# A gated feed-forward layer: block products of seven in place of eight for part of the K tiles, with their weight sums on GpSimd

## The chip, the cores and the metric

The kernel runs on one core of one Trainium2 chip. The metric is the device time of one execution in microseconds; of several runs the median is given. The engines are named as in the profile: PE is TensorE's matmul, PEld its weight load, DVE is VectorE, ACT is ScalarE, POOL is GpSimd, and SP is the queue that issues most DMAs. A q behind a name (SPq) is the engine's sequencer.

## The reference

One decoder layer over 256 tokens of width 2048, in float32. Two groups of token mixers share one projection; then come a gated feed-forward part, which the change touches, and a gated per-layer embedding:

```python
D_FF = 5632
h = rms_norm(x, mix_norm_g[i]); z = h @ w_in[i]
...
x = x + jnp.concatenate([ha, hb], axis=-1) @ w_out[i]
h = rms_norm(x, ffn_norm_g[i])
u = h @ w_up[i]                      # 2048 x 11264
a, g = jnp.split(u, 2, axis=-1)
a = causal_dwconv(a, conv_w[i], conv_b[i])
x = x + (jax.nn.gelu(a, approximate=False) * g) @ w_down[i]   # 5632 x 2048
gate = jax.nn.sigmoid(rms_norm(x, ple_norm_g[i]) @ w_ple_gate[i])
x = x + gate * (p[i].astype(x.dtype) @ w_ple_proj[i])
```

## The kernel before

Every projection streams its weights once from memory, in blocks of 128 partitions by 1024 columns of float32 (512 KB), which hold two K tiles of 128 rows by 512 columns. A product in float32 is made of three fast products: each operand is split into a rounded part hi and a rest lo, and hi x hi, hi x lo and lo x hi are summed in PSUM. For a weight block, ACT casts hi out of the raw block (line 226), DVE subtracts it to get lo (line 228), and PE multiplies (lines 256 to 258; a weight load and a matmul of 512 columns each). For the activations the split is stored once, hi and lo side by side (`split_T`, lines 141 and 142; with a scale lines 144 and 145).

`run_stream` (line 196) is the loop over the list of blocks. It issues the load of a block on SP, eight blocks ahead in this stage (four raw buffers from the pool `w`, four from `ffn`), makes hi and lo three blocks ahead of PE into four buffers of each, and then calls the block's function. After each block `pull(2)` lets waiting side jobs do two steps. Each engine works through its own queue in order; the framework's scheduler may change the order of independent instructions when the program is built.

`token_group` (line 237) makes the blocks of one group of 512 output columns: eight blocks of two K tiles for the up projection, with two PSUM banks, one for each half of the 256 tokens. A block has 2 halves x 2 K tiles x 3 = 12 matmuls. PSUM's eight banks have two tags, `mm` and `aux`, of four each.

In the feed-forward stage, `up(q)` makes for each of eleven q two groups: 512 columns of a, then the same 512 columns of g. `up_evac` (line 689) takes each bank out on ACT with the norm's scale (line 694) and transposes blocks of 32 on DVE (line 695). After the second group `ffn_job(q)` is queued as a side job. It moves the pieces with 16 DMAs on SP (line 707) so that the columns lie on the partitions, does the convolution on ACT (line 728) and DVE (line 731) with its edges on POOL (lines 719 to 725), the GELU on ACT (line 739), the product with g on DVE (line 743), and splits the result into uT (lines 141 and 142). uT holds 24 of the 44 K tiles. The order is up for q = 0 to 5, down over K tiles 0 to 19, up for q = 6 to 10, down over K tiles 20 to 43, so that the first down part doesn't need the last q made before it. In `down`, before the second last block of the first column group all side jobs are run to their end. The last part's evacuation (`resid`, line 653) adds into the residual xs (line 656), transposes the sum on PE (line 153) and squares it on ACT; the gate's projection follows.

POOL runs the convolution's edges, the root of the norms, and at the start of the kernel memsets and the masks' selects (lines 281 and 290). p is loaded by ACT's queue in the mixers' stage (`load_conv`), and its transpose pT is kept until the end.

## Time and profile before

| what | value |
| --- | --- |
| median of 3 runs | 1273.33 us (1273.25 to 1275.93) |
| the profiled execution's own time | 1273.86 us |
| its span, first to last instruction | 1272.0 us |
| granted TensorE clock | 1.000 |
| matmuls of the feed-forward stage begin | 445.8 us (up), 707.9 us (down) |
| their last one begins | 1167.3 us |
| read from memory | 235.40 MB, 187 GB/s over the span |

The span is divided by busy time of each engine. A row of the groups by line and shape reads: line, engine, operation, what is written from what, shapes, count, then total busy us and mean ns of one, then the engine's idle time before it and what ended it. In the timeline a row begins with its start and its length in us, and neighbouring rows of one kind are merged with their count. A window's row has for each engine the busy us and the number of instructions.

### The profile page before, as it was taken

The page shows a single profiled execution, that of the slowest core. Times are in us where ns is not written, and L with a number is a line of the kernel's source. Part 1 is how long each engine was busy: PE and PEld are TensorE (multiplying, and loading weights), DVE is VectorE, ACT ScalarE, POOL GpSimd, SP SyncE. Part 2 cuts the span into 40 slices and gives each one's busy share as a digit, 9 for nine tenths or more (in the row PEclk, how much of TensorE's full clock was granted, in tenths as well). Part 3 has the DMA queues.
Part 4 walks back from the last instruction along what each step waited for, and adds up shares of the span by engine and source line. Part 5 has one row for each costly group of instructions (what it writes and reads, how often), then busy time and mean ns, then how long its engine had stood idle before and what let it go on. Part 6 is the DMA issues. An engine that isn't in the chain of part 4 may idle for free.

```text
span 1272.0 us, 16250 instructions
## 1 busy us (share of the span) xinstructions
PE 1265.6 (99%) x5964; PEld 1068.6 (84%) x5964; DVE 732.6 (58%) x922; ACT 646.6 (51%) x906; POOL 32.2 (3%) x90
## 2 busy tenths in 40 slices
PE   9999999999999999999999999999999999999998
PEld 7899988888888888888888888888888888888888
DVE  6455555646555555667476655447566656555554
ACT  8655455444655444555455533345455545444443
POOL 2000000000000000000000000000000000000000
PEclk9999999999999999999999999999999999999999
DMA  8566756656555576676576666666667667566661
GB/s 285 159 189 188 227 134 205 198 154 183 149 183 182 191 255 189 219 237 217 173 259 227 207 210 197 193 191 227 190 223 235 215 181 247 185 185 196 206 193 49
DMA packets 163520, 252.21 MB, mean 198 GB/s; under 512 B 28169, under 2 KB 59505, under 8 KB 163441
## 3 DMA queue, kind: packets, MB, share of 16 engines
q1 hardware_dynamic: 162560, 250.72, 62.9%
q8 instruction: 47, 0.77, 0.2%
q10 hardware_dynamic: 657, 0.43, 0.1%
q0 software_dynamic: 224, 0.03, 0.1%
q14 instruction: 32, 0.26, 0.1%
HBM read 235.40 MB, written 2.10 MB: 187 GB/s over the span
## 4 chain that ended last, share of the span: by engine, by line
PE 99%; DMA 0%; SPq 0%; DVE 0%; ACT 0%; issue 0%; DVEq 0%
PE tg L257 32%; PE tg L256 32%; PE tg L258 32%; PE xT L153 1%; PE mob L570 0%; DMA xs<-in_x_dram 0%; PE msc L544 0%; PE ob L489 0%; PE qkp L448 0%; PE sc L464 0%; PE rowb L435 0%; PE pt L483 0%; PE msc L548 0%; PE ob L490 0%; PE sc L463 0%; PE hap L604 0%
## 5 line engine op out<-in xcount | busy, mean ns | idle before, releaser
L228 DVE TENSOR_TENSOR lo<-raw,hi 128x1024 fp32r<-128x1024 f32 (+2 forms) x462 | 545.7, 1183 | 471.6 <-ACT hi L226 467.5
L226 ACT CAST hi<-raw 128x1024 fp32r<-128x1024 f32 (+2 forms) x462 | 469.2, 1017 | 514.0 <-PE tg L258 461.0
L258 PE MATMUL tg<-hi,x2T 128*128 128x512 f32 x704 | 274.1, 389 | 0.0
L257 PE MATMUL tg<-lo,x2T 128*128 128x512 f32 x704 | 274.1, 389 | 0.0
L256 PE MATMUL tg<-hi,x2T 128*128 128x512 f32 x704 | 271.2, 389 | 0.0
L256 PE MATMUL tg<-hi,hT 128*128 128x512 f32 (+1 forms) x512 | 186.7, 368 | 0.0
L257 PE MATMUL tg<-lo,hT 128*128 128x512 f32 (+1 forms) x512 | 186.4, 366 | 0.0
L258 PE MATMUL tg<-hi,hT 128*128 128x512 f32 (+1 forms) x512 | 185.9, 366 | 0.0
L256 PEld LDWEIGHTS tg<-hi,x2T 128*128 128x128 f32 x704 | 132.2, 188 | 27.4
L258 PEld LDWEIGHTS tg<-hi,x2T 128*128 128x128 f32 x704 | 132.2, 188 | 27.3
L257 PEld LDWEIGHTS tg<-lo,x2T 128*128 128x128 f32 x704 | 132.2, 188 | 27.3
L257 PE MATMUL tg<-lo,uT 128*128 128x512 f32 x352 | 137.1, 389 | 0.0
L256 PE MATMUL tg<-hi,uT 128*128 128x512 f32 x352 | 137.0, 390 | 0.0
L258 PE MATMUL tg<-hi,uT 128*128 128x512 f32 x352 | 136.9, 389 | 0.0
L257 PEld LDWEIGHTS tg<-lo,hT 128*128 128x128 f32 x512 | 96.3, 188 | 12.6
L256 PEld LDWEIGHTS tg<-hi,hT 128*128 128x128 f32 x512 | 95.9, 188 | 12.3
L258 PEld LDWEIGHTS tg<-hi,hT 128*128 128x128 f32 x512 | 95.9, 188 | 12.1
L258 PEld LDWEIGHTS tg<-hi,uT 128*128 128x128 f32 x352 | 66.1, 188 | 13.7
L257 PEld LDWEIGHTS tg<-lo,uT 128*128 128x128 f32 x352 | 66.1, 188 | 13.6
L256 PEld LDWEIGHTS tg<-hi,uT 128*128 128x128 f32 x352 | 66.1, 188 | 13.5
L257 PE MATMUL tg<-lo,x3T 128*128 128x512 f32 (+1 forms) x160 | 55.5, 347 | 0.0
L258 PE MATMUL tg<-hi,x3T 128*128 128x512 f32 (+1 forms) x160 | 55.5, 347 | 0.0
(207 smaller groups left out, 963.7 us busy)
## 6 DMA issues: line engine op xcount, KB each, us to landing
raw<-in_w_up_dram SPq DMA_DIRECT2D x176, 512.0 KB, 4.3
raw<-in_w_down_dram SPq DMA_DIRECT2D x88, 512.0 KB, 4.7
raw<-in_w_in_dram SPq DMA_DIRECT2D x79, 512.0 KB, 4.2
raw<-in_w_in_dram SPq DMA_DIRECT2D x48, 344.0 KB, 3.5
raw<-in_w_out_dram SPq DMA_DIRECT2D x32, 512.0 KB, 4.3
raw<-in_w_ple_gate_dram SPq DMA_DIRECT2D x32, 512.0 KB, 4.4
Y<-sq SPq DMA_DIRECT2D x176, 64.0 KB, 2.0
xs<-in_x_dram SPq DMA_DIRECT2D x8, 256.0 KB, 7.5
```

The source lines that it names most:

```text
L153: pe.transpose(bk[:, t * P : (t + 1) * P], xs[:, t, k * P : (k + 1) * P], ident)
L226: act.copy(hi[:, :w], raw[:, :w])
L228: dve.tensor_sub(lo[:, :w], raw[:, :w], f32(hi[:, :w]))
L256: pe.matmul(o, ah, hi[:, i, :], start=first, stop=False)
L257: pe.matmul(o, ah, lo[:, i, :], start=False, stop=False)
L258: pe.matmul(o, al, hi[:, i, :], start=False, stop=last)
```

## The change

The up projection is now made in groups of 1024 columns, 512 of a and 512 of g, and the down projection in two groups of 1024. Of such a group, the two token halves, the two column halves and two neighbouring K tiles make a product of 2 x 2 blocks by 2 x 2 blocks. For some pairs of K tiles it is made of seven block products instead of eight (Strassen's scheme in Winograd's form): for the pairs 1, 3 and 5 of 8 in up, and for the second of the two pairs of every q in down. A step called R is one K tile done in the old way, with four outputs (12 matmuls). A pair done in the new way has four steps: o1 (two block products, from the second raw tile as it came), o2 (one, 512 columns), c1 (two) and c2 (two), 21 matmuls in all. Between o2 and c1, POOL makes lo of the 512 columns of o2 and then four sums of 512 columns in place in the pair's two raw tiles, each sum building on earlier ones; c1 takes hi and lo of the first raw tile, c2 of the second.

The four outputs of a group use four banks (D11 to D22), and the products that go into several outputs four more (Q1, Q5, Q6, Q7). After the last c2, `combine` forms the sums of the Q banks on ACT and DVE into four tiles; in up these are scaled on ACT, and at the end DVE adds each D bank with its scale and transposes. The activations need differences of blocks as well: x2E for up (made at the start by POOL, ACT and DVE), and for down four more units per q, which POOL computes. The product with g moves from DVE to POOL.

hi and lo have five buffers of each, four steps ahead of PE, and raw has seven. uT holds four q of eleven units each. The order is now up for q = 0 to 3, down over them, up and down for 4 to 7, up and down for 8 to 10. A down part needs its last q's new units at the step o1 of the last pair; all side jobs are run to their end before that step of the first column group. p is loaded and transposed at the last down group, into the place of x2E.

```diff
-RAW_FFN = 4
-QF = 24
+RAW_FFN = 3
+PARTS_FFN = 1
+S_UP = (1, 3, 5)
+QW = 4
...
+    def halves(raw, w, eng=None):
...
+        act.copy(hi[:, :w], raw[:, :w])
+        last["hi"] = traced()
+        (eng or dve).tensor_tensor(out=lo[:, :w], in0=raw[:, :w], in1=f32(hi[:, :w]), op=ALU.subtract)
+        return hi, lo
...
+    def quad_group(src, seq, unit, tags, mid, end):
...
+                    pe.matmul(st[bk], ah, hi[:, cols], start=first, stop=False)
+                    pe.matmul(st[bk], ah, lo[:, cols], start=False, stop=False)
+                    pe.matmul(st[bk], al, hi[:, cols], start=False, stop=final)
+                    if final and bk[0] == "D":
+                        end(int(bk[1]) - 1, int(bk[2]) - 1, st[bk])
...
+            if kind == "R":
+                p, i = divmod(p, 2)
+                ops = [(f"D{t + 1}{n + 1}", (p, f"{t + 1}{i + 1}"), n) for t in range(NT) for n in range(2)]
+                step = add(ops, [src(2 * p + i)], lambda raws: halves(raws[0], BLK))
+                step.frees = [(step, 0)]
+            elif kind == "o1":
+                opened[p] = step = add([("D12", (p, "E3"), 1), ("D11", (p, "12"), 0)], [src(2 * p), src(2 * p + 1)],
+                                       lambda raws: halves(raws[1], BLK))
+            elif kind == "o2":
+                def split(_, step=opened[p]):
+                    r0, r1 = step.raws
+                    hl = halves(r0, 512, pool)
+                    for dst, oth in ((r0[:, 0:512], r0[:, 512:1024]), (r0[:, 512:1024], r1[:, 512:1024]),
+                                     (r1[:, 512:1024], r0[:, 0:512]), (r1[:, 0:512], r1[:, 512:1024])):
+                        pool.tensor_tensor(out=dst, in0=dst, in1=oth, op=ALU.add)
+                    return hl
+                add([("Q1", (p, "11"), 0)], split=split)
+            elif kind == "c1":
+                add([("Q5", (p, "E5"), 0), ("Q7", (p, "E7"), 1)],
+                    split=lambda _, step=opened[p]: halves(step.raws[0], BLK), frees=[(opened[p], 0)])
+            else:
+                add([("Q6", (p, "E6"), 1), ("D21", (p, "22"), 0)],
+                    split=lambda _, step=opened[p]: halves(step.raws[1], BLK), frees=[(opened[p], 1)], after=closed)
...
+        def combine(st, tiles):
+            t12, t21, t22 = (tiles(c) for c in ("12", "21", "22"))
+            act.copy(t22, st["Q1"])
+            dve.tensor_sub(t21, st["Q6"], t22)
+            dve.tensor_add(t12, st["Q5"], t21)
+            dve.tensor_add(t21, st["Q7"], t21)
+            dve.tensor_add(t22, st["Q7"], t12)
+            return t12, t21, t22
...
             for f in range(4):
-                dve.tensor_mul(u[:, f], c[:, :, :, f].rearrange("p i t r -> p t i r"),
-                               g[:, :, :, f].rearrange("p i t r -> p t i r"))
+                pool.tensor_tensor(out=u[:, f].rearrange("p t (i r) -> p t i r", i=4),
+                                   in0=c[:, :, :, f].rearrange("p i t r -> p t i r"),
+                                   in1=g[:, :, :, f].rearrange("p i t r -> p t i r"), op=ALU.mult)
...
+            differences(e, u[:, 2, 0], u[:, 3, 0], u[:, 2, 1], u[:, 3, 1])
...
-        for q in range(6):
-            up(q)
-        down(0, 20, part_sum)
-        for q in range(6, KF // 4):
-            up(q)
-        down(20, KF, lambda c: resid(c, ssq3, get_x3T, g_ple))
+        for qs in (range(0, 4), range(4, 8), range(8, 11)):
+            for q in qs:
+                up(q)
+            down(qs, qs[-1] == 10)
```

`weave` puts the steps in order. In up it gives R0 R1, then three times the pattern o1 R o2 c1 R c2, then R14 R15. In down over four q it is R R o1 R o2 c1 c2, o1 R o2 c1 c2, o1 R o2 c1 c2, o1 R o2 c1 c2, R R; over three q R R o1 R o2 c1 c2, o1 o2 c1 R c2, o1 o2 c1 c2, R R.

On PE, inside an up group, a block of the program before reads as follows, where the three rows of each bank stand twice in a row, once for each K tile, and are shown once (tg is a group's bank, hi and lo a weight block's parts, x2T the activations):

```order
L256 MATMUL tg_4272<-hi_4207,x2T 128x512
L257 MATMUL tg_4272<-lo_4208,x2T 128x512
L258 MATMUL tg_4272<-hi_4207,x2T 128x512
L256 MATMUL tg_4273<-hi_4207,x2T 128x512
L257 MATMUL tg_4273<-lo_4208,x2T 128x512
L258 MATMUL tg_4273<-hi_4207,x2T 128x512
```

At the same place in the changed program, around an o1 and an o2 (qgD and qgQ are the D and Q banks, x2E the differences):

```order
L313 MATMUL qgD_4122<-hi,x2E 128x512
L313 MATMUL qgD_4118<-hi,x2T 128x512
L313 MATMUL qgQ_4215<-hi,x2T 128x512
L314 MATMUL qgD_4122<-lo,x2E 128x512
L315 MATMUL qgD_4122<-hi,x2E 128x512
L314 MATMUL qgD_4118<-lo,x2T 128x512
L315 MATMUL qgD_4118<-hi,x2T 128x512
```

A bank's three matmuls still follow each other, but the first products with hi of several banks stand ahead, and steps of few matmuls follow each other.

On POOL, one q of the program before has only these five rows (the convolution's edges):

```order
L719 COPY halo_4080<-Y 128x48
L721 COPY halo_4080<-Y 128x8
L722 TENSOR_TENSOR E<-halo_4080,cT 128x64
L724 TENSOR_TENSOR e_5229<-halo_4080,cT 128x32
L725 TENSOR_TENSOR E<-E,e_5229 128x32
```

In the changed program two pairs of an up group stand around them (lo is o2's, raw the sums in place):

```order
L205 TENSOR_TENSOR lo<-raw_5157,hi 128x512
L346 TENSOR_TENSOR raw_5157<-raw_5157 128x512
L346 TENSOR_TENSOR raw_5157<-raw_5157,raw_5159 128x512
L346 TENSOR_TENSOR raw_5159<-raw_5159,raw_5157 128x512
L346 TENSOR_TENSOR raw_5159<-raw_5159 128x512
L205 TENSOR_TENSOR lo<-raw_5188,hi 128x512
L346 TENSOR_TENSOR raw_5188<-raw_5188 128x512
L346 TENSOR_TENSOR raw_5188<-raw_5188,raw_5200 128x512
L877 COPY halo_4068<-Y 128x48
L346 TENSOR_TENSOR raw_5200<-raw_5200,raw_5188 128x512
```

Five operations of 512 columns per pair have come to an engine that had five small ones per q, and each waits for the one before.

On DVE, the same pairs in the changed program (raw_5157 and raw_5159 are the first pair's tiles, raw_5188 and raw_5200 the second's):

```order
L205 TENSOR_TENSOR lo<-raw_5157,hi 128x1024
L205 TENSOR_TENSOR lo<-raw_5179,hi 128x1024
L205 TENSOR_TENSOR lo<-raw_5159,hi 128x1024
L205 TENSOR_TENSOR lo<-raw_5200,hi 128x1024
L205 TENSOR_TENSOR lo<-raw_5218,hi 128x1024
L205 TENSOR_TENSOR lo<-raw_5188,hi 128x1024
L205 TENSOR_TENSOR lo<-raw_5325,hi 128x1024
```

Before, each raw block had one such row, in the order of the loads; now a pair's tiles come up again after POOL's sums, between rows of tiles that need no sum.

More of the change, by code (lines that the diff above doesn't have):

```diff
@@ L109, in layer_kernel @@
     cT = cp.tile([P, 4 * KF], F32, name="cT")
-    pT = bp.tile([P, 2, 512], F32R, name="pT")
     def load_conv(mp):
@@ new lines, in run_stream, with load @@
+    def run_stream(steps, pulls, ramp=False, more=None):
+        nb = len(steps)
+        ring = RAW + (RAW_FFN if more else 0)
+        loads = [(st, i) for st in steps for i in range(len(st.srcs))]
+        index = {(id(st), i): n for n, (st, i) in enumerate(loads)}
+        freed = [False] * len(loads)
+        parts = {}
+        nl = 0
+        deep = AHEAD_SPLIT
+        if more:
+            more_parts.update(pool=more, n=-1)
+            deep += PARTS_FFN
+        def load():
+            nonlocal nl
+            while nl < len(loads) and (nl < ring or freed[nl - ring]):
+                st, i = loads[nl]
+                if i == 0 and st.load is not None:
+                    st.load()
+                src = st.srcs[i]
+                kb, n = src.shape[1], src.shape[2]
+                if nl % ring < RAW:
+                    raw = wp.tile([P, BLK], F32, tag="raw", name=f"raw{nl}", bufs=RAW)
+                else:
+                    raw = more.tile([P, BLK], F32, tag="raw", name=f"raw{nl}", bufs=RAW_FFN)
+                nc.sync.dma_start(out=raw[:, : kb * n].rearrange("p (k n) -> p k n", k=kb), in_=src)
+                st.raws.append(raw)
+                nl += 1
+        split = 0
+        load()
+        for i in range(-1, nb):
+            ahead = min(deep, 1 + i // 2) if ramp else deep
+            while split < min(nb, i + ahead + 1):
+                st = steps[split]
+                if st.prep is not None:
+                    st.prep()
+                parts[split] = st.split(st.raws)
+                for f in st.frees:
+                    freed[index[id(f[0]), f[1]]] = True
+                split += 1
+                load()
@@ L230, in run_stream @@
             if i >= 0:
-                blocks[i][1](*parts.pop(i))
+                steps[i].fn(*parts.pop(i))
                 pull(pulls)
@@ L756, in get_x3T, with tags, weave @@
             return x3T["t"]
-        def part_sum(c):
-            def f(t, b):
-                xc = xs[:, t, c * 512 : (c + 1) * 512]
+        blocks = []
+        turns = [0]
+        def tags():
+            turns[0] ^= 1
+            return ("mm", "aux") if turns[0] else ("aux", "mm")
+        def weave(rs, ss):
+            r = [("R", 2 * p + i) for p in rs for i in range(2)]
+            s = [(kind, p) for p in ss for kind in ("o1", "o2", "c1", "c2")]
+            head, tail = r[:2], r[-2:]
+            r = r[2:-2]
+            seq = []
+            for i, x in enumerate(s):
+                seq.append(x)
+                while r and len(r) * len(s) > (len(s) - 1 - i) * (len(r) + sum(y[0] == "R" for y in seq)):
+                    seq.append(r.pop(0))
+            return head + seq + r + tail
@@ new lines, in down_mid, with f @@
+        def down_mid(c, ends=False):
+            def f(st):
+                if ends and c == 2:
+                    side.append(load_p())
+                xc = [[xs[:, t, (c + n) * 512 : (c + n + 1) * 512] for n in range(2)] for t in range(NT)]
+                dve.tensor_add(xc[0][0], st["Q1"], xc[0][0])
+                t12, t21, t22 = combine(st, tmp)
+                for dst, v, op in ((xc[0][1], t12, ALU.add), (xc[1][0], t21, ALU.subtract), (xc[1][1], t22, ALU.add)):
+                    pool.tensor_tensor(out=dst, in0=dst, in1=v, op=op)
+            return f
@@ L789, in proj_done @@
+        r3, pj, sgn = {}, {}, [0]
         def proj_done(t, b):
```

218 lines of the change are left out of this document (148 added, 70 removed).

## The prediction

> **What bounds the kernel now.** I read the page first: busy shares, the granted clock and the chain that ended last.
>
> ```profile
> PE 1265.6 (99%) x5964; PEld 1068.6 (84%) x5964; DVE 732.6 (58%) x922; ACT 646.6 (51%) x906; POOL 32.2 (3%) x90
> PEclk9999999999999999999999999999999999999999
> PE 99%; DMA 0%; SPq 0%; DVE 0%; ACT 0%; issue 0%; DVEq 0%
> PE tg L257 32%; PE tg L256 32%; PE tg L258 32%; PE xT L153 1%; PE mob L570 0%; DMA xs<-in_x_dram 0%; PE msc L544 0%; PE ob L489 0%; PE qkp L448 0%; PE sc L464 0%; PE rowb L435 0%; PE pt L483 0%; PE msc L548 0%; PE ob L490 0%; PE sc L463 0%; PE hap L604 0%
> ```
>
> TensorE never waits, at full clock; the chain is its three matmul lines. POOL is idle, VectorE busy for 58%. So only fewer matmuls can help, and only while VectorE, ScalarE, POOL and SP deliver in time. Next, the groups by shape, and a window inside the up projection:
>
> ```profile
> 730.00:780.00 50.00, 50.00 (x223) 41.41 (x222) 26.57 (x25) 20.72 (x20) 0.00 (x0) 1.00 0.63 209
> L256 PE MATMUL tg<-hi,x2T 128*128 128x512 f32 x704 | 271.2, 389 | 0.0
> L256 PE MATMUL tg<-hi,uT 128*128 128x512 f32 x352 | 137.0, 390 | 0.0
> L228 DVE TENSOR_TENSOR lo<-raw,hi 128x1024 fp32r<-128x1024 f32 x410 | 501.1, 1224 | 419.9 <-ACT hi L226 415.8 <-DMA Y<-sq 3.0
> L226 ACT CAST hi<-raw 128x1024 fp32r<-128x1024 f32 x410 | 430.0, 1051 | 471.0 <-PE tg L258 421.2 <-DMA raw<-in_w_in_dram 18.4 <-issue 9.1
> ```
>
> The columns of the window are PE, PEld, DVE, ACT and POOL busy. 389 ns is the length of a pipelined matmul, not its price: 223 in 50 us is **0.224 us** each. Up holds 3 x 704 and down 3 x 352, together 3168 or 710 us. VectorE makes one lo per weight block at 1224 ns.
>
> **The matmuls removed.** One up group (512 columns of a and of g) had 16 K tiles x 12 = 192 matmuls. Now ten tiles go the old way (120) and three pairs take 7 x 3 each (63): 183, 41.0 us for 43.0. Eleven groups save 99. A down column group over four q had 192 and has 96 + 84 = 180 (40.4 us for 43.0); over three q 144 becomes 135 (30.3 us). Four and two of these save 66. Together 165 x 0.224 = **37 us**: with TensorE still never waiting, 1273.9 - 37 = 1237. I count from the profiled execution's 1273.86, 0.5 above the median of 1273.33.
>
> **What the other engines get.** Per up group 19 lo of 1024 columns on VectorE instead of 16, on POOL three lo of 512, twelve sums of 512, the four products with g (from VectorE), and four differences of 128. VectorE's rows:
>
> ```profile
> 507.03 1.22 DVE L228 TENSOR_TENSOR lo<-raw,hi 128x1024 fp32r<-128x1024 f32 x1
> 508.16 0.46 DVE L731 SCALAR_TENSOR_TENSOR c<-Y,cT,c 128x240 f32<-128x240 f32 x1
> 504.22 2.89 DVE L731 SCALAR_TENSOR_TENSOR c<-Y,cT,c 128x248 f32<-128x248 f32 x7 [0.57 <-ACT c L728]
> L228 DVE TENSOR_TENSOR lo<-raw,hi 128x512 fp32r<-128x512 f32 x4 | 2.8, 693 | 6.0 <-ACT hi L226 6.0
> L743 DVE TENSOR_TENSOR Y<-c,Y 128x256 f32<-128x256 f32 x44 | 15.8, 421 | 1.9 <-ACT c L739 1.3
> L801 DVE TENSOR_TENSOR sg<-sg,tg 128x128 f32<-128x128 f32 x2 | 0.5, 288 | 0.4 <-ACT sg L800 0.4
> L656 DVE TENSOR_TENSOR xs<-tg,xs 128x512 f32<-128x512 f32 x16 | 10.2, 682 | 0.0
> L695 DVE STREAM_TRANSPOSE sq<-z 128x512 f32<-128x512 f32 x44 | 31.1, 706 | 6.7 <-ACT z L694 6.7
> ```
>
> Back to back a lo costs 1.13 (507.03 to 508.16), about 0.09 less than its length. Operations that read two SBUF tensors, per up group: 19 lo x 1.13 = 21.5; eight of the convolution x 0.40 = 3.2; the four lo of uT (512, 256, 128, 512 columns) 0.69 + 0.42 + 0.29 + 0.69 less 4 x 0.09 = 1.7; edges 0.1. Sum 26.5. Operations with PSUM or one input: four combinations, four evacuations, four transposes, at 0.59 to 0.62 about 7.2. VectorE alone, 34 of 41 us, would hold. ScalarE too: three more casts of 1.05 and three short ones, on 20.7 busy in 50.
>
> POOL's 512-column sums were never run before; its nearest rows are the small ones:
>
> ```profile
> L719 POOL COPY halo<-Y 128x48 f32<-128x48 f32 x11 | 2.5, 223 | 560.8 <-DMA Y<-sq 560.8
> L721 POOL COPY halo<-Y 128x8 f32<-128x8 f32 x11 | 2.1, 189 | 22.7 <-DMA Y<-sq 12.6 <-DVE lo L228 10.1
> L722 POOL TENSOR_TENSOR E<-halo,cT 128x64 f32<-128x64 f32 x11 | 3.2, 293 | 0.9
> L724 POOL TENSOR_TENSOR e<-halo,cT 128x32 f32<-128x32 f32 x11 | 2.6, 240 | 0.0
> L725 POOL TENSOR_TENSOR E<-E,e 128x32 f32<-128x32 f32 x11 | 4.0, 360 | 0.9
> ```
>
> The copies give 0.85 ns an element over a fixed 182 ns; with two inputs 64 against 32 elements give 1.66 (1.81 from the 32 alone). So 512 cost 182 + 512 x 1.66 to 1.81 = 1.03 to 1.11 us; at the copies' rate 0.62. I take 1.05, by the rows of the same operation. Then POOL needs per up group 15 x 1.05 + 4 x 0.62 + 4 x 0.40 + 1.3 (its five old ones) = 21.1 us. Alone, that too would fit into 41.
>
> **The step that decides: do POOL and VectorE run at the same time?** At the start of the kernel POOL runs the same select five times on 128x128 tiles (POOL's timeline and VectorE's of one stretch, and below them two later POOL rows; start, length):
>
> ```profile
> 6.44 0.75 POOL L281 TENSOR_SCALAR_AFFINE_SELECT tri<-tri 128x128 f32<-128x128 f32 x1
> 7.17 0.53 POOL L290 TENSOR_SCALAR_AFFINE_SELECT mk_q<-mk_q 128x128 f32<-128x128 f32 x2
> 6.35 0.69 DVE L228 TENSOR_TENSOR lo<-raw,hi 128x512 fp32r<-128x512 f32 x1
> 7.04 0.88 DVE L145 SCALAR_TENSOR_TENSOR hT<-xT,g_mix,hT 128x256 fp32r<-128x256 f32 x2
> 504.14 0.24 POOL L724 TENSOR_TENSOR e<-halo,cT 128x32 f32<-128x32 f32 x1
> 504.46 0.36 POOL L725 TENSOR_TENSOR E<-E,e 128x32 f32<-128x32 f32 x1
> ```
>
> Beside a lo, which reads two SBUF tensors, one select took 0.75 and ended 0.15 after the lo; beside L145, which reads PSUM and one SBUF tensor, two took 0.53, 0.28 each. L725 points the same way: as many elements as L724, but 360 ns against 240, and it starts at 504.46 in the midst of the L731 that began at 504.22, while L724 had started before it (its output is strided too, so this row alone proves little). So a POOL operation that reads SBUF waits for a VectorE operation that reads two SBUF tensors. I take it that the other order waits as well, which no row shows.
>
> The Trainium skill (SBUF — State Buffer, "Who interferes with whom") states this rule for both orders: the pair of ports that both engines share is locked for a whole instruction, and the later one blocks; the 0.75 against 0.28 us agrees.
>
> So the two times add up. Up group: 26.5 + 21.1 = **47.6 us** against TensorE's 41.0. Down over four q: 20 lo x 1.13 + 20 x 1.05 + three residual sums x 1.05 = 46.8 against 40.4; over three q 15 x 1.13 + 18 x 1.05 = 35.9 against 30.3. Sum 11 x 47.6 + 4 x 46.8 + 2 x 35.9 = 782 us where 710 stood: **+72**. TensorE then waits some 14% of this stretch, a little in every group.
>
> Bounds of this sum. Below: if only the streaming excludes, a lo holds (1224 - 693) / 512 = 1.04 ns an element and POOL 1.66, and an up group comes to 23.7 + 15.6 = 39.3, under 41.0: TensorE sets the end and 1237 returns. Above: if POOL hides beside none of VectorE's 7.2 us of PSUM work (5.3 in a down group), groups cost 54.8, 52.1 and 41.2, 894 us in all: 1457. I take the middle, from the rows' own spacing.
>
> The Trainium skill (GPSIMD Engine Reference, "3.1 Elementwise — side-by-side cycle accounting") gives 4497 ns for a sum of 2048 columns, which makes an estimate of 1.17 us for 512; by it the stretch would be 818 us and the kernel 1385. No run here shows a sum of that size.
>
> **Start and ends of parts.** The first pair's E tiles need x2's sums on POOL, which wait for the tiles of the stage before to be released:
>
> ```profile
> 446.12 0.23 POOL L686 MEMSET halo<- 128x64 f32 x2 [109.97 <-PE tg L258]
> L256 PE MATMUL tg<-hi,x2T x704: 388/389/476, 445.8 to 1033.6; 128*128 128x512 f32 x176
> 1031.36 3.08 SPq L213 DMA_DIRECT2D raw<-in_w_down_dram  x2
> 1034.46 0.69 ACT L694 ACTIVATE z<-tg,rstd_ffn 128x512 f32<-128x512 f32 x1 [0.67 <-PE tg L258]
> 1035.96 10.18 SPq L707 DMA_DIRECT2D Y<-sq  x16
> 1056.53 1.23 DVE L142 TENSOR_TENSOR uT<-Y,uT 128x1024 fp32r<-128x1024 f32 x1
> raw<-in_w_up_dram SPq DMA_DIRECT2D x176, 512.0 KB, 4.3
> pr<-in_p_dram ACTq DMA_DIRECT2D x1, 256.0 KB, 4.4
> ```
>
> From 446.35 POOL has four operations of 512, four short ones and a 0.7 power before the first E tile, then a short cast and lo: ready near 454.5, wanted two tiles (5.4 us) after 445.8. Cost **3 us**. At a part's end the last q's chain took 23.3 us, 1034.46 to 1057.76. It grows by three more transposes at the end (1.9), products on POOL (0.9), differences and their split (0.7), and weight sums queued between (2.1): 29. A down part needs it after five tiles and three pairs, 13.5 + 14.1 = 27.6 us, twice, and after 4 tiles and 2 pairs, 20.2, at the last. That is 1.4 + 1.4 + 8.8, some 9 to 11 us, if TensorE is otherwise full. Where it already waits for weights, the same microseconds pass anyway: 0 in the forecast.
>
> At nothing: SP keeps 16 loads (1.54 each) and 16 Y pieces (10.2) per group, 35 of 41 us; if that cover goes, every group is late by the excess. The load of p, now late on SP, lands in some 4.4 us beside two tiles (5.4 us). The transposes of x3 keep their number. Seven raw buffers for eight: a tile is held from its issue until its lo, 4.3 + 1.05 + 1.2 = 6.6 us, a pair's two some five steps longer, 14, on average 9.4, and seven last 7 x 41 / 16 = 18.
>
> **Forecast:** 1273.9 + 72 + 3 = **1349 us**; its own range is 1300 to 1405.
>
> **Rivals.**
> 1. TensorE stays the bound (not slower, the other side). Speaking for it: each engine alone fits, buffers of five blocks smooth the turns, and the low bound of 39.3 is under 41. Against: POOL's five operations per pair are a chain, and the 0.75 us select. It decides at 41 us for the sum of one group; below it the kernel takes 1237 + 3 + 9 and about 3 for pairs that follow each other in the last part, whose chain of one short cast, three POOL steps, cast and lo (6.7 us) has 5.4 us of matmuls before it: **1252**.
> 2. No overlap at all: VectorE's queue is in order, a lo that waits for POOL's sum holds up the evacuations behind it, and those hold PSUM banks. Price: the upper bound, **1457**.
> That the matmuls aren't fewer can't be: the program has them counted out.
>
> **Chances.** Forecast 0.66, rival 1 0.26, rival 2 0.08. Of the forecast's share about 0.04 ends below today's time and 0.05 level with it. Faster by over 0.2% (about what a measurement of this kernel can tell from no change): 0.30; within: 0.05; slower: 0.65. Range 1247 to 1410: it takes in rival 1, and leaves out most of rival 2, the forecast's top and some of its bottom.
>
> **What would show it.** Right: a POOL row for the 512-column sums whose mean is well above 1.05 us or a lo whose mean is above 1224 ns; TensorE busy near 91%, with its waits put down to lo or hi, and those to POOL's sums; the chain that ended last runs through POOL and VectorE in the up and down stretch. Wrong: sums at 1.05, lo at 1224, TensorE at 98%, and three gaps of a few microseconds at the ends of the parts, which is rival 1. A part-end gap of over 10 us each would mean I undersized the last chain.

## The result, and the profile after

The changed kernel takes **1456.03 us** (median of 4 runs, 1453.88 to 1459.62) against 1273.64 (4 runs, 1273.25 to 1275.93) for the kernel before: a ratio of 1.143, 95% interval 1.140 to 1.146, so 182 us slower. The forecast was 1349, range 1247 to 1410. The direction was right, the size was not. The profiled run took 1453.88 us with a span of 1452.2.

The page of the changed kernel: busy shares, granted clock, and the chain that ended last.

```profile
PE 1316.1 (91%) x5799; PEld 1052.9 (73%) x5799; DVE 972.6 (67%) x1096; ACT 738.0 (51%) x1069; POOL 615.6 (42%) x486
PEclk9999999999999998998999999989999989989999
PE 44%; POOL 24%; issue 12%; DVE 10%; ACT 4%; SPq 4%; DMA 3%; POOLq 0%; DVEq 0%; ACTq 0%
POOL raw L346 13%; PE tg L277 11%; PE tg L278 11%; PE tg L279 11%; POOL lo L205 5%; DVE lo L205 5%; ACT hi L203 4%; SPq L866 3%; POOL Y L901 3%; PE qgD L313 2%; PE qgD L314 2%; DVE sq L889 2%; PE qgD L315 2%; POOL sq L787 1%; DVE t L852 1%
```

TensorE has its 165 matmuls fewer (5799 for 5964), but is busy for 91%, and its clock is no longer full. The chain that was TensorE for 99% is TensorE for 44%; POOL's weight sums (L346) lead it, then come POOL's lo, VectorE's lo and the casts.

The stretch of up and down, from 446 us to the last residual addition, as one window of each kernel (columns: span, then busy time of PE, PEld, DVE, ACT and POOL with instructions, granted clock, share of the DMA engines, GB/s). First the kernel before, then the changed one:

```profile
446.00:1167.80 721.80, 721.80 (x3203) 598.43 (x3202) 429.24 (x497) 359.00 (x408) 14.84 (x58) 1.00 0.66 211
```

```profile
446.00:1344.70 898.70, 772.05 (x3045) 583.77 (x3044) 669.18 (x668) 449.56 (x566) 597.89 (x452) 0.94 0.53 171
```

All of the loss is here: 898.7 - 721.8 = 177 us. At the rate of before (721.8 us for 3168 matmuls) the 3003 left would take 684, so TensorE loses 215 us. VectorE went from 429 to 669 busy, POOL from 15 to 598. Counted from the records of both engines, at least one of the two runs in 868 of the 899 us (97%; before, 438 of 722).

The groups by shape of the changed kernel:

```profile
L205 DVE TENSOR_TENSOR lo<-raw,hi 128x1024 fp32r<-128x1024 f32 x465 | 628.7, 1378 | 344.2 <-ACT hi L203 342.3
L203 ACT CAST hi<-raw 128x1024 fp32r<-128x1024 f32 x465 | 472.9, 1049 | 501.6 <-POOL raw L346 258.5 <-PE tg L279 136.1 <-PE qgD L315 48.4
L346 POOL TENSOR_TENSOR raw<-raw 128x512 f32<-128x512 f32 x110 | 192.1, 1747 | 6.4
L346 POOL TENSOR_TENSOR raw<-raw,raw 128x512 f32<-128x512 f32 x110 | 156.7, 1424 | 6.9 <-DVE lo L205 1.2
L205 POOL TENSOR_TENSOR lo<-raw,hi 128x512 fp32r<-128x512 f32 x55 | 115.3, 2097 | 232.0 <-ACT hi L203 228.4
```

The sums are at 1.75 and 1.42 us on average where the forecast had 1.05, and lo at 1378 ns where it was 1224. ScalarE, whose queue is in order, stands 258 us in front of POOL's sums (its idle time of before was put down to TensorE). The list of waits shows how that reaches TensorE:

```profile
ACT hi L203 <- POOL raw L346: 258.5, 81, 8.2
PE qgQ L313 <- ACT hi L203: 68.6, 42, 5.2
PE qgD L313 <- ACT uT L791: 12.1, 1, 12.1
```

(us in total, times, longest.) TensorE waits for the casts of summed tiles (products qgQ), and once, at the end of a part, for the last q.

One more cost shows in TensorE's timeline, right behind such a wait (start, length):

```profile
470.05 0.39 PE L315 MATMUL qgQ<-hi,x2T 128*128 128x512 f32 x1
474.74 1.22 PE L313 MATMUL qgQ<-hi,x2E 128*128 128x512 f32 x2 [4.30 <-ACT hi L203]
...
478.41 0.63 PE L314 MATMUL qgQ<-lo,x2E 128*128 128x512 f32 x1
478.84 0.63 PE L315 MATMUL qgQ<-hi,x2E 128*128 128x512 f32 x1
...
480.40 0.40 PE L314 MATMUL qgD<-lo,x2T 128*128 128x512 f32 x1
480.63 0.40 PE L315 MATMUL qgD<-hi,x2T 128*128 128x512 f32 x1
```

After 4.30 us of waiting the matmuls start 0.43 us apart until 480.1, then 0.23 again. In the window 477 to 480 the granted clock is 0.50. Some 145 spacings of the stretch lie at 0.40 to 0.48 us, 0.2 us too many in each, so 29 us are lost; before there were none. The Trainium skill (TensorE: Matmul & The Clock Gate, "Part 1: The HAM clock gate") says that the clock halves after an idle window of about 3.4 us and that matmuls of 512 columns then start 426.7 ns apart; this trace agrees on the spacing, with 426 to 427. It does not bear out 3.4 us as the length of one wait: at 577 and at 1010 us half speed follows spacings of no more than 2.2 us, with others of about 1 us beside them.

### The profile page after: what moved, and what is told of

It is laid out like the page before. It is cut to its first block, busy times and chain, and to the rows that moved or that the text cites. A ratio compares the mean times of both kernels' runs of the same rounds, so it can differ in the third digit from the quotient of the medians.

```text
span 1452.2 us, 16956 instructions
## 1 busy us (share of the span) xinstructions
PE 1316.1 (91%) x5799; PEld 1052.9 (73%) x5799; DVE 972.6 (67%) x1096; ACT 738.0 (51%) x1069; POOL 615.6 (42%) x486
## 3 DMA queue, kind: packets, MB, share of 16 engines
q1 hardware_dynamic: 151568, 250.98, 55.7%
## 4 chain that ended last, share of the span: by engine, by line
PE 44%; POOL 24%; issue 12%; DVE 10%; ACT 4%; SPq 4%; DMA 3%; POOLq 0%; DVEq 0%; ACTq 0%
POOL raw L346 13%; PE tg L277 11%; PE tg L278 11%; PE tg L279 11%; POOL lo L205 5%; DVE lo L205 5%; ACT hi L203 4%; SPq L866 3%; POOL Y L901 3%; PE qgD L313 2%; PE qgD L314 2%; DVE sq L889 2%; PE qgD L315 2%; POOL sq L787 1%; DVE t L852 1%
## 5 line engine op out<-in xcount | busy, mean ns | idle before, releaser
L205 DVE TENSOR_TENSOR lo<-raw,hi 128x1024 fp32r<-128x1024 f32 (+2 forms) x517 | 673.9, 1327 | 395.8 <-ACT hi L203 393.9
L205 POOL TENSOR_TENSOR lo<-raw,hi 128x512 fp32r<-128x512 f32 x55 | 115.3, 2097 | 232.0 <-ACT hi L203 228.4
L314 PE MATMUL qgD<-lo,x2T 128*128 128x512 f32 x506 | 201.8, 399 | 7.0 <-DVE lo L205 7.0
L315 PE MATMUL qgD<-hi,x2T 128*128 128x512 f32 x506 | 199.4, 395 | 0.0
L346 POOL TENSOR_TENSOR raw<-raw 128x512 f32<-128x512 f32 x110 | 192.1, 1747 | 6.4
L313 PE MATMUL qgD<-hi,x2T 128*128 128x512 f32 x506 | 174.0, 414 | 4.8 <-ACT hi L203 4.8
L346 POOL TENSOR_TENSOR raw<-raw,raw 128x512 f32<-128x512 f32 x110 | 156.7, 1424 | 6.9 <-DVE lo L205 1.2
L313 PEld LDWEIGHTS qgD<-hi,x2T 128*128 128x128 f32 x506 | 98.6, 199 | 32.9 <-ACT hi L203 13.9
L314 PEld LDWEIGHTS qgD<-lo,x2T 128*128 128x128 f32 x506 | 98.1, 194 | 31.8 <-DVE lo L205 11.0
L315 PEld LDWEIGHTS qgD<-hi,x2T 128*128 128x128 f32 x506 | 97.2, 192 | 20.7
L314 PE MATMUL qgD<-lo,uT 128*128 128x512 f32 x242 | 98.9, 410 | 5.3 <-DVE lo L205 4.9
L313 PE MATMUL qgD<-hi,uT 128*128 128x512 f32 x242 | 85.6, 416 | 15.8 <-ACT uT L791 12.1
L315 PE MATMUL qgD<-hi,uT 128*128 128x512 f32 x242 | 97.2, 402 | 0.0
```

What stands on the lines that cost most here:

```text
L205: (eng or dve).tensor_tensor(out=lo[:, :w], in0=raw[:, :w], in1=f32(hi[:, :w]), op=ALU.subtract)
L313: pe.matmul(st[bk], ah, hi[:, cols], start=first, stop=False)
L314: pe.matmul(st[bk], ah, lo[:, cols], start=False, stop=False)
L315: pe.matmul(st[bk], al, hi[:, cols], start=False, stop=final)
L346: pool.tensor_tensor(out=dst, in0=dst, in1=oth, op=ALU.add)
```

## The experiments

Four accounts were tried. **A**, the one of the prediction: operations of POOL that read SBUF and operations of VectorE that read two SBUF tensors exclude each other, and the added times set the pace. **B**: POOL's operations are too long by themselves. **C**: the rest of the change (order, wide groups, three parts, ring of raw tiles). **D**: the chain of one pair (short cast, POOL's lo, four sums, cast) through ScalarE's queue. Times below are single runs beside a run of the kernel before (1273.65 to 1275.63), except for v1 to v3; runs of one kernel differ by 0.2 to 0.5%, 3 to 6 us. Each edit is shown in part; `...` stands for lines left out.

### e8: the frame without pairs

The list of pairs is empty in up and in down, and all tiles are taken as R. Without pairs there are no Q banks and no differences; the evacuation goes through ACT again, as before. As built, p was transposed behind the first products that read it, so the first column group of the last projection ran on zeros; its matmuls are the same in number.

```diff
-S_UP = (1, 3, 5)
+S_UP = ()
+S_DN = ()
...
```

> The changed kernel without any pair in seven products: all tiles the old way, so TensorE has the 3168 matmuls of before; column groups of 1024, down in three parts and the product with g on POOL stay, and the last group's tiles come last in each part. The 62 us that the kernel without sums stood above 1237 are either of this frame (the rest of the change): then this one stands as far above 1274, 1310 to 1340; or they are of the pairs' short steps and the extra lo: then 1274 to 1290. Theory A gives 29 us of shared time per up group against 43 of matmuls, so TensorE never waits for it.

1278.55 us. Its page:

```profile
PE 1269.0 (99%) x5964; PEld 1069.1 (84%) x5964; DVE 730.4 (57%) x909; ACT 650.9 (51%) x928; POOL 91.5 (7%) x135
PEclk9999999999999999999999999999999999999999
```

The stretch takes 724.3 us for 721.8. Groups of 1024 columns, three parts, seven raw tiles and the product on POOL cost 2.5 us together: this much of C falls, and what was put at nothing in the prediction for these parts holds while the pairs are away. The order of the pairs' short steps, which C names too, is not in this run.

### e1: pairs without the sums

```diff
-                    for dst, oth in ((r0[:, 0:512], r0[:, 512:1024]), (r0[:, 512:1024], r1[:, 512:1024]),
-                                     (r1[:, 512:1024], r0[:, 0:512]), (r1[:, 0:512], r1[:, 512:1024])):
-                        pool.tensor_tensor(out=dst, in0=dst, in1=oth, op=ALU.add)
```

> The changed kernel without the four weight sums of each pair (220 on POOL in all); the products that need them take the blocks as loaded. Prices from the changed kernel's trace, undisturbed: POOL's 512-column operation 1.29 us, VectorE's lo 1.13. Theory A (operations of POOL that read SBUF and operations of VectorE that read two SBUF tensors exclude each other, both ways, so their times add and set the pace): 220 x 1.29 = 284 us leave the shared sum of about 865, which falls to 581, below TensorE's 673 of this stretch, so TensorE is the bound again: 1245 to 1275. Theory B (POOL's chain alone is too slow, whatever VectorE does): the same, 1245 to 1275. Theory C (the order of the work on ScalarE and VectorE, the ring of seven raw tiles, or the chains at the ends of the parts, not the sums): above 1400.

1299.34 us, above the 1245 to 1275 of A and B alike. So the sums carry most of the loss (155 of 182 us), but not all: TensorE loses 746.3 - 684 = 62 us with no sum in the program. VectorE is busy for 606 of these 746 us. By the starts of the matmuls, 22 of the 62 us are lost in the up groups and 41 in the down groups.

### e2: POOL's lo on VectorE

```diff
-                    hl = halves(r0, 512, pool)
+                    hl = halves(r0, 512)
```

> The changed kernel with the third lo of a pair (512 columns, 55 in all) on VectorE in place of POOL. Theory A (the times of both engines add): POOL gives up 55 x 1.29 = 71 us, VectorE takes on 55 x 0.60 = 33, and the end comes by the difference: 38 us earlier, 1416 (1400 to 1430). Theory B (POOL alone sets the pace): 71 us earlier, 1383 or less. Theory C (order, ring, part ends): within 10 us of 1454.

1434.91 us: 19 earlier than the profiled 1453.88, where A said 38 and B 71. Taking work from POOL does not give back its length (B falls), and gives back half of what the bare sum of A does; the time is 5 us above A's range.

### e3: sums that only write

```diff
-                    for dst, oth in ((r0[:, 0:512], r0[:, 512:1024]), (r0[:, 512:1024], r1[:, 512:1024]),
-                                     (r1[:, 512:1024], r0[:, 0:512]), (r1[:, 0:512], r1[:, 512:1024])):
-                        pool.tensor_tensor(out=dst, in0=dst, in1=oth, op=ALU.add)
+                    for r in (r0, r0, r1, r1):
+                        pool.memset(r, 1.0)
```

> The changed kernel with each of the 220 weight sums on POOL replaced by a write of a constant over the whole raw tile (1024 columns, no operand read from SBUF), so the products that need sums get constants. POOL stays in the chain of every pair with the same waits, and is expected to be busy about as long per pair (some 1 us each). Theory A (it is reading SBUF on POOL beside two SBUF operands on VectorE that excludes): the writes run beside VectorE's lo, VectorE's mean lo falls back to about 1.22 us, 1245 to 1300. Theory B (POOL's chain by its length and its waits): 1400 to 1460. If the writes are blocked as well, lo stays near 1.38 us and the time above 1400, and A would have to be widened to any access of SBUF.

1359.92 us, between all bounds given. POOL's writes, one line of the kernel (minimum, median and maximum in ns):

```profile
L345 POOL MEMSET raw<- x220: 942/953/965, 445.9 to 1235.0; 128x1024 f32 x110
```

Not one of 220 is lengthened beside VectorE, while the sums spread from 1.26 to 2.30 us. So it is reads that exclude. The Trainium skill (SBUF — State Buffer, "Who interferes with whom") says this too: an instruction of GpSimd that only writes SBUF does not contend with a VectorE instruction of two SBUF inputs. Yet 121 us of TensorE's loss stay though no sum is read.

This remainder is no measure of a kernel without exclusion. The writes need none of each other's results, and in the program as built many stand earlier in POOL's queue than the sums did, some ahead of POOL's lo. There POOL waits for VectorE's lo to have read the tile (the groups by shape of e3):

```profile
L345 POOL MEMSET raw<- 128x1024 f32 x220 | 206.7, 953 | 297.1 <-DVE lo L205 293.0
```

109 of these 293 us pass before the stretch, 184 in it; the sums of the changed kernel waited 1.2 us for VectorE's lo. POOL's lo, the product with g and the differences still read, too: VectorE's lo is at 1.31 us on average here, above its 1.22.

### e4: the disputed cost alone, in the kernel before

```diff
                 dve.tensor_sub(lo[:, :w], raw[:, :w], f32(hi[:, :w]))
+                if more:
+                    pool.tensor_tensor(out=dummy[:, :w], in0=raw[:, :w], in1=dummy[:, :w], op=ALU.add)
...
```

> The kernel before, with one POOL operation added for each of the 264 weight blocks of up and down: a running sum of the raw block (1024 columns) into a scratch tile of its own, whose result is used by nothing. Nothing waits for it but the raw tile's next load, eight blocks on. Estimate of its length alone: 2 x 1.29 less one fixed part, 2.3 to 2.6 us, against 2.69 us of matmuls per block. Theory A (the times add): 1.13 + 2.35 + 0.4 of the other work per block in up = 3.9 us against 2.69, and 3.5 in down: 176 x 1.2 + 88 x 0.8 = 280 us slower, about 1550 (1500 to 1620), with lo well above 1.22 us on average. Theory B (independent engines): POOL keeps up with 2.69, and the time stays at 1274 to 1285.

1549.61 us, where A said about 1550 (1500 to 1620). That it is met to the microsecond is chance: 37 more such sums than expected belong to the last stage, which grew by 14 us. VectorE's and POOL's timelines of one place:

```profile
600.69 3.36 DVE L231 TENSOR_TENSOR lo<-raw,hi 128x1024 fp32r<-128x1024 f32 x1
603.97 2.57 DVE L739 SCALAR_TENSOR_TENSOR c<-Y,cT,c 128x240 f32<-128x240 f32 x1
606.47 3.39 DVE L231 TENSOR_TENSOR lo<-raw,hi 128x1024 fp32r<-128x1024 f32 x1
609.78 0.70 DVE L703 STREAM_TRANSPOSE sq<-z 128x512 f32<-128x512 f32 x1
```

```profile
598.12 24.74 POOL L233 TENSOR_TENSOR dummy<-raw,dummy 128x1024 f32<-128x1024 f32 x9
```

Here POOL works without a gap, and each VectorE operation with two SBUF operands waits for one whole POOL operation: lo takes 3.4 for 1.22 us, and a convolution step of 240 columns, 0.46 before, takes 2.57. The transpose, with one operand, keeps its 0.70. This shows the order of blocking that no row of before had: **VectorE waits for POOL as well**. 101 times lo follows lo so, and the pair of lo and sum takes 3.34 us; with lo's own 1.13 that leaves 2.21 us in which the sum of 1024 columns keeps lo out, while the shortest of these sums start 2.44 to 2.51 us apart.

### e5: the third step of a pair set apart from the second

The changed order in up is R R, then o1 o2 R R c1 c2 for each pair, then R R; it was o1 R o2 c1 R c2 in the middle, with the sums of o2 directly ahead of the c1 that reads them.

```diff
-            for i, x in enumerate(s):
-                seq.append(x)
...
+            for p in ss:
+                seq += [("o1", p), ("o2", p)] + r[:n] + [("c1", p), ("c2", p)]
+                r = r[n:]
...
```

> The changed kernel with another order of steps in a group: the second step of a pair, which issues the sums, no longer stands directly ahead of the third, which needs them; two whole tiles (one in down) stand between, 5.4 us of matmuls. Nothing else differs, and POOL and VectorE have the same work. Theory A in its strict form (the added times of the two engines set the pace; some 865 us of the stretch's 899): 1440 to 1460. Theory D (the chain of one pair is too long for the steps ahead of it: short cast, POOL's lo, four sums, cast, and ScalarE's queue stands still meanwhile): TensorE's waits in front of the products that need sums go, 86 us in the changed kernel's list of waits, and the half-speed matmuls behind them, some 30 us: 1340 to 1380.

1449.54 us, as A has it; D had 1340 to 1380. The sums of the changed kernel, by their operands, and below them those of this run:

```profile
L346 POOL TENSOR_TENSOR raw<-raw x110: 1259/1732/2267, 449.8 to 1328.5; 128x512 f32<-128x512 f32 x110
L346 POOL TENSOR_TENSOR raw<-raw,raw x110: 1256/1292/2297, 452.5 to 1327.1; 128x512 f32<-128x512 f32 x110
L346 POOL TENSOR_TENSOR raw<-raw x110: 1257/2150/2381, 452.0 to 1325.8; 128x512 f32<-128x512 f32 x110
L346 POOL TENSOR_TENSOR raw<-raw,raw x110: 1256/1339/6051, 453.7 to 1324.4; 128x512 f32<-128x512 f32 x110
```

The median of the first kind rises from 1.73 to 2.15 us: these sums meet VectorE more often. TensorE's waits for casts of summed tiles halve (68.6 to 34.6 us), but 28 of these 34 us come back in its other waits of the stretch (54 to 82). Where sums and lo alternate (38 neighbouring blocked sums here), one pair takes 2.23 us: 1.13 for lo and **1.10 for the sum**.

### e6 and e10: the same order, writes in place of sums

e6 has e5's order with the writes of e3; e10 adds a second write, so that POOL is busy as long as with real sums (0.954 + 0.338 = 1.29 us).

```diff
                     for r in (r0, r0, r1, r1):
                         pool.memset(r, 1.0)
+                        pool.memset(r[:, 0:288], 1.0)
```

> The order of steps of e5_steps_apart, and the sums replaced by POOL writes of a constant as in e3_sums_write_only (products that need sums get constants). Theory D: the 61 us by which the write-only kernel stood above the one without sums (1360 against 1299) are the pair's chain, and go: 1285 to 1315. Theory A alone has no price for the chain: about 1360.

> e6_steps_apart_write_only with a second short write of 288 columns behind each of its 220, so that POOL is busy about 1.3 us for each sum as in the changed kernel (products that need sums get constants). Order of steps and waits are those of e5_steps_apart (1449.5), which has real sums. Theory A (reading SBUF beside two SBUF operands is what costs): the extra 0.35 us x 220 = 77 us of POOL run beside VectorE and are hidden in the steps between: 1331 to 1350. Theory B (POOL's length): near 1449, at least above 1400.

e6: 1330.72 us, between D's 1285 to 1315 and A's 1360; e10: 1369.94, and neither A (1331 to 1350) nor B (above 1400) has it. e10 is **80 us** faster than e5 with the same steps and sums that only write. e10 and e6 differ in POOL's length: 39 of the 74 us come through (220 x 0.338), although no sum reads. e6 against e3, the order of the steps, is 29 us.

```profile
L345 POOL MEMSET raw<- 128x1024 f32 x220 | 205.9, 954 | 176.6 <-DVE lo L205 166.4
```

The 80 us are the reads' price only as far as the rest is alike. It isn't quite: as in e3, e10's writes stand earlier in POOL's queue, and POOL waits 57 us of the stretch (166.4 less the 109 before it) for VectorE's lo in front of them, where e5's sums waited 3. How much of that reaches TensorE, and so by how much 80 is off, was not tried; of e6's 29 us the share of the chain is open for the same reason (184 us of such waits in e3, 44 in e6). And with POOL's lo and the product still reading, e10 is not free of the exclusion: POOL's lo takes 1.7 us on average, 1.28 at its shortest.

### e7, e9 and e11: the sums on VectorE

e7 moves the four weight sums to VectorE; e9 moves POOL's lo, the product with g and the residual sums as well; e11 is e9 in e5's order.

```diff
-                        pool.tensor_tensor(out=dst, in0=dst, in1=oth, op=ALU.add)
+                        dve.tensor_tensor(out=dst, in0=dst, in1=oth, op=ALU.add)
```

> The changed kernel with the four weight sums of each pair on VectorE in place of POOL; the third lo of a pair stays on POOL. Theory A: POOL's 220 x 1.29 = 284 us become 220 x 0.60 = 132 us on VectorE; the shared sum goes from 865 to 713 us, near TensorE's 673 to 681 for this stretch, and the chain of a pair falls from 6.5 to 3.7 us: 1300 to 1340. If POOL were slow by itself and VectorE free beside it: below 1290. If VectorE's queue, in order, becomes the new wait: above 1360.

> The changed kernel with all its weight and activation sums that read SBUF on VectorE: the weight sums, the pair's third lo, the product with g and the residual sums; POOL keeps the four short differences and the halo rows. The order of steps is the changed kernel's. VectorE alone, at its own undisturbed spacing (1024-column lo 1.13, 512-column operations 0.60): up group 19 x 1.13 + 15 x 0.60 + 1.4 + 5.0 + 7.2 of PSUM work = 44.1 us, with the rest of POOL's time up to 47; down 41.7 and 33 us per column group. Theory A (each POOL operation is paid on the shared ports at more than twice VectorE's price for the same work): 1283 to 1316, against 1366 with only the sums moved. If POOL's remaining 166 us ran beside VectorE: no better than 1366, since VectorE only gets more to do.

> e9_all_on_dve (1375) with two whole tiles (one in down) between the second and third step of a pair. POOL has almost nothing to do. If e9 was held by the pair's chain through ScalarE's and VectorE's queues (ScalarE waited 154 us for the sums there): 1290 to 1335, VectorE's own sum being 44 to 47 us per up group. If it was VectorE's total time: 1365 to 1375.

1365.59, 1374.76 and 1373.69 us. e7 came out 26 us above A's range and in the one for VectorE's queue as the new wait, e9 59 above A's and where it was put if POOL's remaining work ran beside VectorE; so POOL's price in A was not what held these runs. e11 lies where "VectorE's total time" was expected. The stretch in e11:

```profile
446.00:1265.20 819.20, 743.27 (x3058) 579.52 (x3057) 752.82 (x1007) 450.69 (x566) 108.59 (x117) 0.96 0.59 188
```

VectorE is busy for 753 of 819 us, 92%, with POOL almost out of the way. The 44.1, 41.7 and 33 us per group, from spacings of single operations, add up to 718 and were too few: 753 us are 1.10 times TensorE's 684. So with the sums on VectorE this change cannot end before VectorE does.

### e12: one operand taken from VectorE's lo

e5 with the 1024-column lo of this stage and the next as a copy of raw (354 operations).

```diff
-        (eng or dve).tensor_tensor(out=lo[:, :w], in0=raw[:, :w], in1=f32(hi[:, :w]), op=ALU.subtract)
...
+            dve.tensor_copy(lo[:, :w], raw[:, :w])
...
```

> e5_steps_apart (1449.5) with VectorE's 1024-column lo made by a copy of the raw block, one SBUF operand, in place of raw minus hi (the products with lo get other values; all counts and waits on raw stay, the wait on hi goes). POOL's sums are real. Theory A, if only two SBUF operands exclude: POOL's sums fall to 1.29 us on average, lo is not lengthened, 1300 to 1350. If a copy excludes as well for its length: the copy's own row tells its price; at 0.6 to 1.1 us in place of 1.13 the shared sum falls by 0 to 160 us: 1330 to 1449.

1320.97 us, 129 less than e5. The copy and the sums (minimum, median, maximum):

```profile
L206 DVE CAST lo<-raw x354: 644/694/1823, 437.5 to 1302.1; 128x1024 fp32r<-128x1024 f32 x177
```

```profile
L349 POOL TENSOR_TENSOR raw<-raw x110: 1265/1303/1852, 450.2 to 1202.3; 128x512 f32<-128x512 f32 x110
L349 POOL TENSOR_TENSOR raw<-raw,raw x110: 1255/1617/1808, 452.2 to 1200.7; 128x512 f32<-128x512 f32 x110
```

The time lies in the range for "only two SBUF operands exclude", but the rows speak against it: sums beside nothing but copies still reach 1.85 us instead of some 2.3, and the copy 1.82. So a copy excludes too, for its own 0.6 us. The run got 214 us of VectorE's time back (500 busy for e5's 714), shorter blocks with it, and a lo that no longer waits for hi; it can't tell these apart.

### v1 to v3: fewer pairs

One pair of eight in up (v3: two), every other q in down and never a part's last q, whose tiles come last; product on VectorE, three whole tiles between the second and third step. v1 keeps sums and third lo on POOL; v2 and v3 have them on VectorE.

```diff
-S_UP = (1, 3, 5)
+S_UP = (3,)
+S_DN = (0, 2, 4, 6, 8)
...
```

> Fewer pairs: in up one of eight pairs of K tiles in seven products instead of three, in down one per two q instead of one per q, and none in a part's last q, whose four tiles come last; sums and third lo on POOL, the product with g on VectorE, three whole tiles between the second and third step of a pair. 63 matmuls fewer than the kernel before, 14 us. Shared time of an up group by the measured prices: about 36 us, 43 with VectorE's PSUM work, against 42.3 of matmuls. Theory A: TensorE nearly bound, 1264 to 1285.

> As v1_one_pair_pool, with the sums, the third lo and the residual sums on VectorE too. Up group: VectorE 35.8 us with its PSUM work, POOL at most 3, against 42.3 of matmuls, so TensorE is the bound: 1273.9 - 14.1 + 4 (start and frame) = 1264 (1260 to 1270), faster than the kernel before.

> As v2_one_pair_dve with two pairs in up (96 matmuls fewer than before, 21.5 us). VectorE 40 us per up group, with POOL's rest up to 43, against 41.7 of matmuls: if VectorE keeps up 1257, if it is the bound in part 1260 to 1285. It tells how near to full VectorE may run before TensorE starts to wait and its clock halves.

v1: 1280.29 us (4 runs; ratio to before 1.0050, 1.0036 to 1.0064). v2: 1278.24 (5 runs; 1.0041, 1.0027 to 1.0055). v3: 1288.78 (5 runs; 1.0126, 1.0107 to 1.0145). v1 is in its range, v2 (1260 to 1270) and v3 (at most 1285) are not. None beats the kernel before, though v1 and v2 have 63 matmuls fewer and v3 96. In v1 and v2 an up group in the midst of a part takes 42.8 to 43.3 us, TensorE's own rate for 189 matmuls, and the first one 43.8. Of what v2 loses, 18 us fall in the down groups, the largest waits (10.6 us in four) at two ends of parts.

The stretch in all of this, from windows like those above; the loss is the stretch less 0.2278 us (721.8 / 3168) for each matmul, and the last column is the share in which VectorE or POOL runs, counted from the records:

| run | stretch, us | VectorE busy | POOL busy | TensorE's loss | either runs |
|---|---|---|---|---|---|
| before | 721.8 | 429 | 15 | 0 | 61% |
| e8, no pairs | 724.3 | 427 | 74 | 3 | 62% |
| v1, one pair, POOL | 727.0 | 570 | 251 | 20 | 84% |
| v2, one pair | 726.4 | 601 | 46 | 19 | 85% |
| v3, two pairs | 735.2 | 652 | 52 | 35 | 90% |
| e1, no sums | 746.3 | 606 | 254 | 62 | 88% |
| e12, lo by copy | 767.1 | 500 | 514 | 83 | 92% |
| e6, apart, writes | 773.9 | 609 | 446 | 90 | 93% |
| e3, writes | 804.8 | 598 | 437 | 121 | 92% |
| e7, sums on VectorE | 810.4 | 745 | 269 | 126 | 97% |
| e10, writes as long | 815.1 | 608 | 493 | 131 | 93% |
| e11, all on VectorE | 819.2 | 753 | 109 | 135 | 94% |
| e9, all on VectorE | 820.5 | 754 | 92 | 136 | 94% |
| e2, lo on VectorE | 881.7 | 683 | 486 | 198 | 97% |
| e5, steps apart | 896.0 | 714 | 649 | 212 | 95% |
| changed | 898.7 | 669 | 598 | 215 | 97% |

The loss does not follow the last column: at 92% it is 83 or 121 us, at 97% 126 or 215. And in the midst of an up part, where v1's share is 84% and v2's 88%, TensorE loses nothing.

## Why the prediction was wrong, point by point

**TensorE was the bound, and 37 us of matmuls go.** Right: 5799 matmuls, and e8 shows that the frame without pairs does not disturb TensorE.

**POOL and VectorE exclude each other, both ways.** Right, and now shown: the unlengthened writes of e3 and the lengthened lo and convolution of e4. The 80 us between e5 and e10 agree, with the reservation made there.

**A 512-column sum takes POOL 1.05 us.** Wrong as a length: beside no VectorE operation with two SBUF operands it is 1.29 us (72 sums, 1.256 to 1.310), and two follow each other in 1.37. The estimate of 1.17 by the Trainium skill (GPSIMD Engine Reference, "3.1 Elementwise — side-by-side cycle accounting") was short as well. As the time for which a sum keeps lo out it was nearly right: 1.10 in e5. The forecast's own addition, with its 293 operations of 512 columns, gives 797 us at 1.10 and 853 at 1.29 where it had 782; the records of the changed kernel have 829 us in which POOL or a two-operand VectorE operation runs. So this term was some 47 us short.

**The step that failed: "So the two times add up", as the whole of the cost.** The forecast took this sum as the pace and let all else hide beside it: VectorE's PSUM work, the pair's chain, the ends of parts. It took the middle between its bounds; the two selects that ran at 0.28 us each beside L145 show that VectorE's PSUM work can lie beside POOL, not that it always does. In the changed kernel's own stretch, by the records, the 899 us are 829 in which POOL or a two-operand VectorE operation runs, 39 with VectorE on other work alone, and 30 with neither; the forecast had 782, 0 and 0, and 3 for the start. So of the 114 us by which it was short, some 47 are the sum itself and some 70 what it put at nothing, less the 3. That TensorE would lose only by the sum fails in e1 as well: with no weight sum it loses 62 us, while VectorE is busy for only 81%. TensorE's loss in the changed kernel is 215 us where the forecast had 785 - (710 - 37) = 112.

**How the rest gets through.** The two engines hand work to each other through ScalarE's queue. A piece of the chain that ended last, in order of time, and a row of VectorE's timeline behind it:

```profile
801.37 1.48 POOL lo L205
802.85 0.04 issue
802.89 0.02 POOLq L346
802.91 0.02 issue
802.93 2.15 POOL raw L346
...
805.16 2.16 POOL raw L346
807.32 0.07 issue
807.39 1.30 POOL raw L346
808.70 0.07 issue
808.77 2.16 POOL raw L346
810.93 0.02 issue
810.95 1.06 ACT hi L203
```

```profile
810.44 7.37 DVE L205 TENSOR_TENSOR lo<-raw,hi 128x1024 fp32r<-128x1024 f32 x6 [0.67 <-ACT hi L203]
```

From POOL's lo to the cast behind the last sum 9.6 us pass, three of four sums blocked by lo's of other steps. ScalarE's casts stand in order: it waited 6.05 us for the second sum, cast the pair's first tile at 807.35 and one more at 809.35, and from 810.95 five in a row. The work then comes at once: VectorE has six lo's in a row from 810.4, and sums of the Q banks behind them. At this place the steps split ahead nearly cover it (TensorE waits 0.5 us); over the stretch it waits 68.6 us for the casts of summed tiles. Which part is the in-order queue and which the number of buffers of hi and lo was not tried.

**Start, ends of parts.** By the starts of TensorE's matmuls the first up group takes 53.2 us and the next three 54.0, 55.7 and 53.6, where 47.6 were put: the 3 us of the start can't be told from the rest. The forecast put the ends of parts at nothing because TensorE would wait anyway; one wait of 12.1 us for the last q, in the last part, stands alone in the list of waits, and e10's list has 19.1 us in four. The 9 to 11 us that the prediction had worked out and dropped were near that.

**The clock.** No term had it: 29 us of half-speed matmuls. How much of it is hidden beside the waits for the two engines can't be told from these runs.

**Rival 1** (1252, TensorE stays the bound) is out: even with sums that read nothing (e10) or none on POOL (e11) the time is 1370 to 1374. **Rival 2** (1457, no overlap) has the time, by luck: its 894 us for the stretch are sums at 1.05 and no time with both engines idle, while the 899 measured hold 47 us more of shared time and 30 with neither; and of 118 us in which VectorE worked on other than two SBUF operands, 79 did lie beside POOL, which this rival denied.

**The signs that were named.** Sums well above 1.05, lo above 1224, TensorE at 91%, waits on hi and those on POOL's sums, and a chain through POOL and VectorE: all came. They tell that the two engines set the pace, but not by how much. The 91% is no confirmation of the sum: the forecast meant full-speed matmuls in 1349 us, and what came is 1316 us busy of 1452, more than the 1266 before though 165 matmuls are gone, because PE's records count half-speed matmuls as busy, and each one that stands alone at its full 0.39 us.

## What to carry to other kernels

Before work is moved from a full engine to idle ones, add up the time of those that will feed it as one resource where they exclude each other. Where that left room, as in the midst of v1's and v2's up parts, TensorE lost nothing; where the sum was above TensorE's time, as in the changed kernel, the loss was about twice what the sum said (215 us for 112). Three products saved in 24 were worth 0.67 us and cost two engines six operations of 1.1 to 1.4 us (four sums, two lo's) and more behind them. A sum of such prices bounds the time from below only; work that fails to overlap and waits for chains come on top (some 70 us here). A run that is to take the contention away and keep the chain, as e10 was, has to keep the order of every queue as well: here the writes moved in POOL's, and the two could not be parted cleanly.

## What was not expected of the hardware

- A blocked operation waits for the other's whole instruction, so short ones suffer most: 0.46 us became 2.57 behind 1024-column sums (e4).
- In turns with lo (1.13 us), POOL's sum adds 1.10 us (e5), though two sums alone start 1.37 us apart; at 1024 columns it adds 2.21 of some 2.48 (e4). So about 0.27 us of each did not keep VectorE out.
- VectorE's copy of 1024 columns, one SBUF operand, takes 0.64 us at its shortest and still excludes POOL's reads (e12). The Trainium skill (SBUF — State Buffer, "Who interferes with whom") says that copies can contend in a mode that uses both ports; e12 agrees.
